# Order and SBUF byte offsets of the stationary tiles in the gate/up and q/k units of a fused decoder block

## Chip, cores and metric

The kernel runs on one core of a Trainium2 chip. The metric is the device time of one execution in microseconds (us). Three timed executions of the kernel before gave 1644.78, 1644.87 and 1646.24 us, so the median is 1644.87 us.

## What is computed

One decoder block on 256 tokens and 2048 channels, all in float32. The parts that matter here are the projections that make q and k of both attention branches, and the gated MLP:

```python
proj = x @ w_in                       # columns: GLA q/k/v/gate, FoX q/k/v, merge gates
...
def conv_gated_mlp(x, w_gate, w_up, conv_w, conv_b, w_down):
    g = causal_dwconv(x @ w_gate, conv_w, conv_b)
    h = jax.nn.gelu(g) * (x @ w_up)
    return h @ w_down
```

`w_gate` and `w_up` are 2048 x 5632. The q and k columns of `w_in` that concern us are 4 x 1024.

## The kernel before, in words

**Precision by parts.** Every float32 weight and activation is split into a high part (rounded to the matmul's fp32r format) and a low part (the rest). A product is taken as high x high + high x low + low x high. ScalarE makes the high part of a weight block with one copy (L132), VectorE makes the low part with one subtraction (L256).

**Units.** The weights come from HBM in units of 128 x 2048 floats, 284 of them, numbered u in the order in which they are used. `prep` loads a unit as two halves, and makes two high tiles and two low tiles of 128 x 1024. It runs three units ahead of the use. The high tiles rotate through six buffers of the pool `rhi`, the low tiles through six of `rlo`; each buffer has 1088 columns, 64 more than a tile, and the function `place(u)` says at which column the tile begins in its buffer (high, low). A column has 4 bytes. So `place` alone sets the byte offset of the tiles, and nothing else moves with it.

**Stationary weights.** Two kinds of units use the weight tiles as the stationary operand (the one that LDWEIGHTS loads): the 32 q/k units (u = 0 to 31) and the 88 gate/up units of the MLP (u = 136 to 223, gate and up in turn, so that odd u are up). All others use them as the moving operand. `w_unit` does one such unit. For each of 16 blocks of 128 weight rows (kts) there is a high matmul, L321: stationary high weights, moving 512 columns (256 high activations and 256 low ones); and a low matmul, L326: stationary low weights, moving the 256 high activations, added to the second half of the same PSUM bank. I call a high and the low behind it a pair. Each matmul comes with its own weight load, which the profile shows as PEld.

**The turn.** A unit whose number is in `TURN` has another order: six pairs, then the ten remaining lows in a row, then the ten remaining highs in a row. Before, this is unit 139 alone, the first gate/up unit behind the three units 136 to 138, which the step after the first LayerNorm does in another way (`w_phase`).

**Order around it.** In the q/k stage a `tick` in the middle of each unit lets one step of the attention or of the GLA levels put a few small matmuls or transposes between the pairs. In the MLP stage nothing stands between the units on TensorE: each gate or up unit is followed at once by the next. ScalarE and VectorE evict the PSUM bank, make the convolution, GELU and product (L363, L1458 to L1486), and the conversions of coming units.

Offsets in bytes before: q/k units 96 (high) and 240 (low); units 136 to 138 0 and 64; unit 139 0 and 208; units 140 to 223 64 and 16; all others 0 and 0. The program's tile addresses begin at a multiple of 256 bytes in every buffer, and the moving activations do too.

Of the kernel before, what the change touches and what calls it, by code (L numbers as in the profile page):

```python
# [35 lines left out]
GAPS = (96, 64, 80)  # L36


TURN = (139,)


def place(u):
    if u < 32:
        return 24, 60
    if u < 136 or u >= 224:
        return 0, 0
    if u < 139:
        return 0, 16
    return (0, 52) if u in TURN else (16, 4)


P_STAT = 5000
# [37 lines left out]
def tile_block(ctx: ExitStack, tc: tile.TileContext, wu, wfv, wpp, xT_in, x_in, pT_in, wlr,  # L90
# [28 lines left out]
    def t1(name):  # L119
        return sm.tile([P, 256], F32, tag="t1", bufs=6, name=name)  # L120
# [43 lines left out]
    def lo_tile(u, name):  # L164
        o = place(u)[1]
        return rlo.tile([P, 1088], F32R, tag="lo", name=f"lo{name}")[:, o:o + 1024]

    def hi_tile(u, name):
        o = place(u)[0]
        return rhi.tile([P, 1088], F32R, tag="hi", name=f"hi{name}")[:, o:o + 1024]  # L170
# [144 lines left out]
    def w_unit(ps, hi, lo, act, kts, first, last, tick=None):  # L315


        n = len(kts)

        def high(i, end=False):  # L320
            nc.tensor.matmul(ps, lhsT=hi[i // 8][:, i % 8 * P:i % 8 * P + P],  # L321
                             rhs=act[kts[i] // 4][:, kts[i] % 4, :], start=first and i == 0,
                             stop=last and end)

        def low(i, end=False):
            nc.tensor.matmul(ps[:, 256:512], lhsT=lo[i // 8][:, i % 8 * P:i % 8 * P + P],  # L326
                             rhs=act[kts[i] // 4][:, kts[i] % 4, 0:256], start=False,
                             stop=last and end)

        turn = n_used[0] - 1 in TURN  # L330
        pairs = 6 if turn else n
        for i in range(pairs):
            high(i)
            low(i, i == n - 1)
            if tick is not None:
                tick(i)
        for i in range(pairs, n):
            low(i)
        for i in range(pairs, n):
            high(i, i == n - 1)  # L340

    def w_phase(ps, hi, lo, act, t, kts, part=slice(None)):

# [141 lines left out]
    for u in range(8):  # L485
        hi, lo = fvu[u]
        for j in range(2):
# [8 lines left out]
            for t, i, c in seq:  # L496
                o, n = fch[c]
# [35 lines left out]
    for t in range(2):  # L533
        for c, (o, n) in enumerate(fch):
            n = min(n, 1024 - o)
# [143 lines left out]
    for n in range(16):  # L679
        h, j = n // 2, n % 2  # L680
        hi, lo = unit()

        ps = (mxtile if n == 0 else mmtile)(f"psf{'qk'[j]}{h}")
        w_unit(ps, hi, lo, xT, range(16), True, True,
               tick=lambda i: pull(1) if i == 7 else None)
        if n % 8 == 0:
            fqk[h // 4] = s8([P, 4, 2, 256], name=f"fqk{h // 4}")
        comb(ps, fqk[h // 4][:, h % 4, j], (P ** -0.5, 1.0)[j])
        if n >= 1:
            pull(1, parks)  # L690
# [105 lines left out]
    for n in range(16):  # L796
        nm, dst, sc = (("q", gq, 1.0 / 16.0), ("k", gk, 1.0))[n // 2 % 2]
        h, c = n // 4, n % 2
        hi, lo = unit()
        ps = mmtile(f"ps{nm}{2 * h + c}")  # L800
        w_unit(ps, hi, lo, xT, range(16), True, True,
               tick=lambda i: pull(1, mixers if n < 4 else levels) if i == 7 else None)
        comb(ps, dst[:, h, :].rearrange("p (t c n) -> p t c n", t=2, c=2)[:, :, c, :], sc)
        if n >= 4:
            pull(1)
        if n >= 1:
            pull(1, parks)
# [346 lines left out]
    for n in range(PSM1, 32):  # L1154
        if n in (26, 28):
            i = n // 2 - 13
# [282 lines left out]
    def gate_up(name):  # L1439
        if first:  # L1440
            return first.pop(0)
        hi, lo = unit()
        ps = mmtile(name)
        w_unit(ps, hi, lo, x1T, range(16), True, True)
        return ps

    for n in range(NF):
# [18 lines left out]
        u = t1("up")  # L1466
# [318 lines left out]
```

## Time and profile before

| | us |
|---|---|
| median of three timed executions | 1644.87 |
| the profiled execution, its own time | 1644.61 |
| its span, first to last instruction | 1642.8 |
| q/k units, first high matmul to the first of the next stage | 54.1 to 247.1 |
| gate/up units by `w_unit`, first to last | 847.0 to 1318.8 |

The page gives busy shares and the chain of waits that ends last; a busy TensorE is not a TensorE at its peak, because matmuls overlap. What tells the speed of a stretch that TensorE fills without a gap is the distance from the start of one matmul to the start of the next like it, read from the timeline, whose first column is the start in us from the span's begin and whose second is the duration.

### The profile page before, as it was taken

The numbers are of one execution on the slowest core, as the hardware profiler recorded it, in microseconds if no ns is written. First come the engines' busy times: TensorE is split into PE (matmuls) and PEld (weight loads), VectorE is DVE, ScalarE is ACT, GpSimd is POOL, SyncE is SP. The second block draws the span as 40 slices with busy tenths as digits, with TensorE's granted clock in tenths as the row PEclk, the third lists the DMA queues.
The fourth block names the chain that finished last, engine by engine and source line by source line (L and its number), as shares of the span: only waits on it lengthen the run. The fifth ranks groups of instructions, "written<-read, shape, count | busy, mean of one in ns | idle before, by whom it ended". The sixth has DMA issues, their size and how long they took to land.

```text
span 1642.8 us, 23489 instructions
## 1 busy us (share of the span) xinstructions
PE 1636.9 (100%) x8422; PEld 1402.9 (85%) x8422; DVE 1356.2 (83%) x1964; ACT 910.6 (55%) x1277; POOL 91.2 (6%) x244
## 2 busy tenths in 40 slices
PE   9999999999999999999999999999999999999998
PEld 9988888888888888888898888888888888888887
DVE  7687899788989857779987888888877688988787
ACT  6655555456666654446564444555555456566554
POOL 0000000000000000000010111110111000000000
PEclk9999999999999999999999999999999999999999
DMA  8799799878888768889756898888776679899474
GB/s 325 285 370 346 288 380 361 294 262 307 306 332 306 247 203 310 302 333 373 290 198 195 311 335 319 315 308 302 272 245 216 207 264 335 310 352 350 160 261 157
DMA packets 114838, 477.81 MB, mean 291 GB/s; under 512 B 13032, under 2 KB 14320, under 8 KB 95136
## 3 DMA queue, kind: packets, MB, share of 16 engines
q1 hardware_dynamic: 105216, 417.57, 71.2%
q0 software_dynamic: 9504, 58.73, 9.0%
q8 instruction: 66, 1.08, 0.2%
q14 instruction: 52, 0.43, 0.1%
HBM read 417.53 MB, written 58.73 MB: 290 GB/s over the span
## 4 chain that ended last, share of the span: by engine, by line
PE 99%; DVE 0%; ACT 0%; POOL 0%; issue 0%; ACTq 0%
PE psm L1006 11%; PE dn L868 10%; PE psu L321 10%; PE psg L321 9%; PE psa L1006 5%; PE psu L326 5%; PE psg L326 5%; PE dn_p L868 4%; PE wo L868 3%; PE gr L868 3%; PE gv L868 3%; PE fv L499 3%; PE pg L380 3%; PE psb L1006 3%; PE gr_p L868 2%; PE gv_p L868 2%
## 5 line engine op out<-in xcount | busy, mean ns | idle before, releaser
L256 DVE TENSOR_TENSOR lo<-raw,hi 128x1024 fp32r<-128x1024 f32 x456 | 551.7, 1220 | 138.5 <-ACT hi L132 137.2
L132 ACT ACTIVATE hi<-raw 128x1024 fp32r<-128x1024 f32 x456 | 476.9, 1057 | 301.7 <-DMA raw<-in_wu_dram 70.9
L321 PE MATMUL psu<-x1T,hi 128*128 128x512 f32 x688 | 239.5, 392 | 0.0
L321 PE MATMUL psg<-x1T,hi 128*128 128x512 f32 x672 | 234.9, 392 | 0.0
L326 PE MATMUL psu<-x1T,lo 128*128 128x256 f32 x688 | 191.3, 280 | 0.0
L326 PE MATMUL psg<-x1T,lo 128*128 128x256 f32 x672 | 188.6, 281 | 0.0
L1006 PE MATMUL psm<-hi,xT 128*128 128x512 f32 x512 | 163.1, 393 | 0.0
L321 PEld LDWEIGHTS psu<-x1T,hi 128*128 128x128 f32 x688 | 129.2, 188 | 28.2
L321 PEld LDWEIGHTS psg<-x1T,hi 128*128 128x128 f32 x672 | 126.2, 188 | 27.6
L132 ACT ACTIVATE hi_b<-raw 128x512 fp32r<-128x512 f32 x112 | 93.4, 842 | 71.6 <-DMA raw<-in_wu_dram 21.6
L326 PEld LDWEIGHTS psu<-x1T,lo 128*128 128x128 f32 x688 | 128.6, 188 | 0.0
L326 PEld LDWEIGHTS psg<-x1T,lo 128*128 128x128 f32 x672 | 126.2, 188 | 0.4 <-DVE lo L256 0.3
L230 DVE TENSOR_TENSOR lo_b<-raw,hi_b 128x512 fp32r<-128x512 f32 x112 | 105.1, 953 | 16.7 <-ACT hi_b L132 16.4
L174 DVE TENSOR_TENSOR td<-td 128x512 f32<-128x512 f32 x172 | 117.8, 685 | 0.9
L1006 PEld LDWEIGHTS psm<-hi,xT 128*128 128x128 f32 x512 | 96.3, 188 | 19.5
L230 DVE TENSOR_TENSOR lo_t<-td,hi_t 128x1024 fp32r<-128x1024 f32 x86 | 101.7, 1220 | 12.9 <-ACT hi_t L132 12.1
L132 ACT ACTIVATE hi_t<-td 128x1024 fp32r<-128x1024 f32 x86 | 88.1, 1053 | 28.0 <-DMA td<-td 15.5
L1006 PE MATMUL psm<-lo,xT 128*128 128x512 f32 x256 | 99.9, 390 | 0.0
L868 PE MATMUL dn<-hi,hC 128*128 128x512 f32 x352 | 97.9, 389 | 0.0
L1006 PE MATMUL psa<-hi,oT 128*128 128x512 f32 x256 | 81.2, 392 | 0.0
L868 PEld LDWEIGHTS dn<-hi,hC 128*128 128x128 f32 x352 | 66.0, 188 | 13.7
L1006 PEld LDWEIGHTS psa<-hi,oT 128*128 128x128 f32 x256 | 48.1, 188 | 9.9
(414 smaller groups left out, 3128.8 us busy)
## 6 DMA issues: line engine op xcount, KB each, us to landing
raw<-in_wu_dram SPq DMA_DIRECT2D x525, 512.0 KB, 6.2
td<-in_wu_dram SPq DMA_DIRECT2D x43, 1024.0 KB, 8.9
td<-td POOLq DMA_DIRECT2D x43, 1024.0 KB, 7.5
td<-td SPq DMA_DIRECT2D x43, 1024.0 KB, 8.0
hS<-sd SPq DMA_DIRECT2D x11, 1024.0 KB, 8.7
raw<-in_wu_dram SPq DMA_DIRECT2D x43, 256.0 KB, 7.7
fvraw<-in_wfv_dram SPq DMA_DIRECT2D x13, 524.0 KB, 6.9
sd<-hs POOLq DMA_DIRECT2D x24, 256.0 KB, 5.6
```

Of the source, the lines that this page charges most:

```text
L132: return nc.scalar.activation(o, i, AF.Copy, bias=0.0, scale=scale)
L174: sub = lambda o, a, b: nc.vector.tensor_tensor(o, a, b, ALU.subtract)
L230: nc.vector.tensor_tensor(lo, src, hi.bitcast(F32), ALU.subtract)
L256: i = nc.vector.tensor_tensor(lo, raw, hi.bitcast(F32), ALU.subtract)
L321: nc.tensor.matmul(ps, lhsT=hi[i // 8][:, i % 8 * P:i % 8 * P + P], rhs=act[kts[i] // 4][:, kts[i] % 4, :], start=first and i == 0, stop=l ...
L326: nc.tensor.matmul(ps[:, 256:512], lhsT=lo[i // 8][:, i % 8 * P:i % 8 * P + P], rhs=act[kts[i] // 4][:, kts[i] % 4, 0:256], start=False, s ...
L380: nc.tensor.matmul(bs[j][:, 0:m], lhsT=x, rhs=v[:, o:o + m], start=first and i == 0, stop=last and i == 2)
L499: nc.tensor.matmul(fbk[t][c][:, 0:n], lhsT=x, rhs=w[:, o:o + n], start=kt == 0 and i == 0, stop=kt == 15 and i == 2)
L868: nc.tensor.matmul(ps[:, e], lhsT=x, rhs=w, start=k == 1, stop=k == total.get(id(ps), 3 * ns))
L1006: nc.tensor.matmul(ps[t], lhsT=x, rhs=v, start=first and i == 0 and j == 0, stop=last and i == 3 and j == 2)
```

## The change

`place` gives the q/k units the offsets of the MLP units: 64 and 16 bytes. `TURN` becomes every fourteenth unit from 139 to 223: 139, 153, 167, 181, 195, 209 and 223, all of them up units. Their tiles stand at 0 and 240 bytes. And the end of a turn has another order: nine lows in a row, ten highs in a row, and then the last low.

```diff
-TURN = (139,)
+TURN = range(139, 224, 14)
 def place(u):
-    if u < 32:
-        return 24, 60
-    if u < 136 or u >= 224:
+    if 32 <= u < 136 or u >= 224:
         return 0, 0
-    if u < 139:
+    if 136 <= u < 139:
         return 0, 16
-    return (0, 52) if u in TURN else (16, 4)
+    return (0, 60) if u in TURN else (16, 4)
...
         for i in range(pairs):
             high(i)
             low(i, i == n - 1)
...
-        for i in range(pairs, n):
+        for i in range(pairs, n - 1):
             low(i)
         for i in range(pairs, n):
-            high(i, i == n - 1)
+            high(i)
+        if turn:
+            low(n - 1, True)
```

On TensorE, unit 139 (an up unit, PSUM tile psu1) ends before like this, and unit 140 (psg2) begins; hi139_0 is the first of its two high tiles, lo139_1 the second of its low tiles, and x1T0 to x1T3 are the four activation tiles:

```order
L326 MATMUL psu1_8057<-x1T1_7632,lo139_0_7830 128x256 x3
L326 MATMUL psu1_8057<-x1T2_7633,lo139_1_7836 128x256 x4
L326 MATMUL psu1_8057<-x1T3_7634,lo139_1_7836 128x256 x4
L321 MATMUL psu1_8057<-x1T1_7632,hi139_0_7828 128x512 x2
L321 MATMUL psu1_8057<-x1T2_7633,hi139_1_7834 128x512 x4
L321 MATMUL psu1_8057<-x1T3_7634,hi139_1_7834 128x512 x4
L321 MATMUL psg2_8109<-x1T0_7631,hi140_0_7860 128x512
L326 MATMUL psg2_8109<-x1T0_7631,lo140_0_7862 128x256
```

The same place in the changed kernel (the lines are two lower):

```order
L324 MATMUL psu1_8057<-x1T1_7632,lo139_0_7830 128x256 x3
L324 MATMUL psu1_8057<-x1T2_7633,lo139_1_7836 128x256 x4
L324 MATMUL psu1_8057<-x1T3_7634,lo139_1_7836 128x256 x3
L319 MATMUL psu1_8057<-x1T1_7632,hi139_0_7828 128x512 x2
L319 MATMUL psu1_8057<-x1T2_7633,hi139_1_7834 128x512 x4
L319 MATMUL psu1_8057<-x1T3_7634,hi139_1_7834 128x512 x4
L324 MATMUL psu1_8057<-x1T3_7634,lo139_1_7836 128x256
L319 MATMUL psg2_8109<-x1T0_7631,hi140_0_7860 128x512
L324 MATMUL psg2_8109<-x1T0_7631,lo140_0_7862 128x256
```

One low matmul has moved behind the ten highs, so that unit 140 now follows a low and not a high.

Unit 153 (psu8), before, has sixteen pairs; here are its ninth pair, its last, and the first of unit 154 on TensorE:

```order
L321 MATMUL psu8_8868<-x1T2_7633,hi153_1_8736 128x512
L326 MATMUL psu8_8868<-x1T2_7633,lo153_1_8738 128x256
...
L321 MATMUL psu8_8868<-x1T3_7634,hi153_1_8736 128x512
L326 MATMUL psu8_8868<-x1T3_7634,lo153_1_8738 128x256
L321 MATMUL psg9_8924<-x1T0_7631,hi154_0_8801 128x512
L326 MATMUL psg9_8924<-x1T0_7631,lo154_0_8803 128x256
```

In the changed kernel it ends as a turn:

```order
L324 MATMUL psu8_8868<-x1T1_7632,lo153_0_8732 128x256 x3
L324 MATMUL psu8_8868<-x1T2_7633,lo153_1_8738 128x256 x4
L324 MATMUL psu8_8868<-x1T3_7634,lo153_1_8738 128x256 x3
L319 MATMUL psu8_8868<-x1T1_7632,hi153_0_8730 128x512 x2
L319 MATMUL psu8_8868<-x1T2_7633,hi153_1_8736 128x512 x4
L319 MATMUL psu8_8868<-x1T3_7634,hi153_1_8736 128x512 x4
L324 MATMUL psu8_8868<-x1T3_7634,lo153_1_8738 128x256
L319 MATMUL psg9_8924<-x1T0_7631,hi154_0_8801 128x512
L324 MATMUL psg9_8924<-x1T0_7631,lo154_0_8803 128x256
```

Nine of its low matmuls have moved ahead of ten of its highs; the number of matmuls is the same. Units 167, 181, 195, 209 and 223 change in the same way. On ScalarE three conversions change places with a neighbour, on VectorE two; GpSimd and the DMA queue of SyncE keep their order.

## The prediction

> **What bounds the kernel now.** I read the page first: the first rows, the clock row and the chain of waits that ended last.
>
> ```profile
> span 1642.8 us, 23489 instructions
> ...
> PE 1636.9 (100%) x8422; PEld 1402.9 (85%) x8422; DVE 1356.2 (83%) x1964; ACT 910.6 (55%) x1277; POOL 91.2 (6%) x244
> ...
> PEclk9999999999999999999999999999999999999999
> ...
> PE 99%; DVE 0%; ACT 0%; POOL 0%; issue 0%; ACTq 0%
> ```
>
> TensorE is never without work, its clock is granted in full, and 99% of the chain is TensorE. So time can only come from how closely the matmuls follow each other. A group's mean duration doesn't tell that, since matmuls overlap; the timeline does, by the starts. In the MLP, from unit 157 (the first rows) to the last pair of unit 223:
>
> ```profile
> 947.21 0.39 PE L321 MATMUL psu<-x1T,hi 128*128 128x512 f32 x1
> 947.44 0.28 PE L326 MATMUL psu<-x1T,lo 128*128 128x256 f32 x1
> 947.56 0.39 PE L321 MATMUL psu<-x1T,hi 128*128 128x512 f32 x1
> ...
> 1318.49 0.39 PE L321 MATMUL psu<-x1T,hi 128*128 128x512 f32 x1
> ```
>
> 67 units of 16 pairs begin between these, so the first and last high are 1071 pairs apart: 371.28 / 1071 = 346.7 ns a pair, without one break. The q/k stage has the same pairs with other byte offsets (96 and 240). Two of its stretches, each with 23 pairs from the first row to the second:
>
> ```profile
> 238.90 0.39 PE L321 MATMUL psk<-xT,hi 128*128 128x512 f32 x1
> ...
> 246.80 0.39 PE L321 MATMUL psk<-xT,hi 128*128 128x512 f32 x1
> ...
> 223.84 0.40 PE L321 MATMUL psq<-xT,hi 128*128 128x512 f32 x1
> ...
> 231.92 0.39 PE L321 MATMUL psq<-xT,hi 128*128 128x512 f32 x1
> ```
>
> The first takes 7.90 / 23 = 343.5 ns a pair, the second 8.08 / 23 = 351.3 ns, with the same instructions, shapes and offsets. So a run of pairs settles into one of several rhythms and keeps it until something breaks in; offsets and the place where it starts decide which. This is all that the change can touch: 1408 pairs altogether, where 1 ns is 1.4 us.
>
> **The change part by part.** No matmul, load or conversion is added or removed. Four effects are left.
>
> *The q/k offsets.* By the starts, 128 of the 512 pairs lie in stretches like the second and the rest in stretches like the first, so the mean is 0.75 x 343.5 + 0.25 x 351.3 = 345.5 ns. What 64 and 16 bytes give, the MLP shows. The run to look at is the one where this rhythm was broken and began anew:
>
> ```profile
> 941.78 0.19 PEld L326 LDWEIGHTS psg<-x1T,lo 128*128 128x128 f32 x1 [0.35 <-DVE lo L256]
> ...
> 942.01 0.39 PE L321 MATMUL psg<-x1T,hi 128*128 128x512 f32 x1
> ...
> 943.40 0.39 PE L321 MATMUL psg<-x1T,hi 128*128 128x512 f32 x1
> ```
>
> At 941.4 TensorE waited 0.35 us for a low tile. The four pairs from 942.01 took 1.39 us, 347.5 ns each, and by 947.21 the 346.7 ns was back. So I take 346.7 for q/k too: 512 x 1.2 ns = +0.6 us. Each of the 32 units is broken in the middle by the other stage's matmuls, and a restart cost under 0.01 us here: 0.2 us more. Bounds: all pairs at 351.3 would be 512 x 5.8 = +3.0 us; all at the least I can build, below, -2.8 us.
>
> *The form of the turn.* Unit 139 and what follows it, before:
>
> ```profile
> 847.05 0.39 PE L321 MATMUL psu<-x1T,hi 128*128 128x512 f32 x1
> ...
> 848.34 0.28 PE L326 MATMUL psu<-x1T,lo 128*128 128x256 f32 x1
> 848.45 0.40 PE L321 MATMUL psu<-x1T,hi 128*128 128x512 f32 x1
> ...
> 849.03 1.45 PE L326 MATMUL psu<-x1T,lo 128*128 128x256 f32 x11
> 850.31 2.46 PE L321 MATMUL psu<-x1T,hi 128*128 128x512 f32 x10
> 852.61 0.39 PE L321 MATMUL psg<-x1T,hi 128*128 128x512 f32 x1
> ...
> 853.30 0.39 PE L321 MATMUL psg<-x1T,hi 128*128 128x512 f32 x1
> ...
> 854.35 0.39 PE L321 MATMUL psg<-x1T,hi 128*128 128x512 f32 x1
> ...
> 858.16 0.39 PE L321 MATMUL psu<-x1T,hi 128*128 128x512 f32 x1
> ...
> 863.71 0.39 PE L321 MATMUL psg<-x1T,hi 128*128 128x512 f32 x1
> ```
>
> The turn unit takes 852.61 - 847.05 = 5.56 us, the next 5.55, the one after 5.55, against 16 x 346.7 = 5.547. The lows in a row come every (850.31 - 849.03) / 11 = 116 ns, the ten highs every 230. So six new turns, each with the restart behind it, cost about 6 x 0.02 = +0.1 us. Moving one low to the end changes nothing in that sum. How a row at 240 bytes in place of 208 goes is not in the trace: the bounds are the pairs' own, 16 x (351.3 - 346.7) = +0.07 us and about as much below nothing, for each of seven turns: +-0.5 us. I take 208's value, the nearest.
>
> *The rhythm behind a turn.* This is the large term: units 140 to 223 without the six new turns are 78 units, 1248 pairs, and each now follows, somewhere ahead of it, a turn that ends on a low. Where these settle is not shown by any row, as no row has this start. The bounds: slow, 351.3, is +4.6 ns a pair, +5.7 us. Fast: the shortest distances seen are 113 ns for a low (848.34 to 848.45, to two digits) and 227 ns for a high in runs without lows (below), 340 ns in all, -6.7 ns a pair, -8.4 us; with the q/k pairs at 340, 512 x 5.5 = -2.8 us.
>
> ```profile
> 604.06 0.39 PE L1006 MATMUL psa<-hi,oT 128*128 128x512 f32 x1
> ...
> 625.82 0.39 PE L1006 MATMUL psb<-hi,ofTr 128*128 128x512 f32 x1
> ```
>
> (96 matmuls of 512 columns in 21.76 us: 226.7 ns each.) Between the bounds I take no change, 346.7, because the trace has two starts of this offset pair, one behind ten highs (852.61: five pairs in 1.74 us, 348 ns, and then 346.7) and one behind a wait that left the pairs out of step (942.01), and both end in the same rhythm within some four pairs. It seems to draw in whatever starts near it.
>
> *Tiles kept longer.* In a turn the first high tile is read until pairs 7 and 8 of the highs row, behind nine lows: 6 x 0.347 + 9 x 0.116 + 2 x 0.23 = 3.6 us into the unit instead of 8 x 0.347 = 2.8. So its buffer comes free 0.8 us later, for the ScalarE copy of the unit three further on. That copy's group over the MLP, and the only row in the list of TensorE's waits over the span:
>
> ```profile
> L132 ACT ACTIVATE hi<-raw 128x1024 fp32r<-128x1024 f32 x168 | 176.0, 1057 | 104.0 <-issue 41.6 <-DMA raw<-in_wu_dram 39.7 <-PE psu L321 15.9
> ...
> PE warm_ps L142 <- DVE warm L139: 1.2, 1, 1.2
> ```
>
> ScalarE does wait for up units' tiles (15.9 us in all), but it converts three units ahead, 3 x 5.5 us, and the list of TensorE's own waits holds nothing but the start; the only late tile is that of 941.8. The unit that was late there is 156, which is three behind the new turn 153. But its copy was not held by a buffer: it stood behind a GELU copy on ScalarE that waited for VectorE.
>
> ```profile
> 939.11 0.42 ACT L1464 ACTIVATE yc<-yc 128x256 f32<-128x256 f32 x1 [2.71 <-DVE yc L1463]
> 939.43 2.94 ACT L132 ACTIVATE hi<-raw 128x1024 fp32r<-128x1024 f32 x3
> ```
>
> So the cover holds; if it didn't, that wait would grow from 0.35 to at most 1.2 us. The few neighbours that change places on ScalarE and VectorE are one instruction of about 1 us each and are hidden in the same way. I put this at nothing, with +0.8 us as the upper bound.
>
> **The sum:** +0.6 + 0.2 + 0.1 = +0.9 us on the profiled execution's own 1644.61 (span 1642.8 and 1.8 around it), 1645.5. The median of the runs shown lies 0.26 us higher, so the forecast for a median is 1645.6 to 1645.8; I take 1645.6. What a measurement of this kernel can tell from no change is about 0.2%, 3.3 us, so this counts as within it.
>
> **A rule against the change.** The trace shows 343.5, 346.7 and 351.3 ns for the same pair. The Trainium skill, TensorE: Matmul & The Clock Gate, Part 2 (the step on LDWEIGHTS), says that TensorE has two independent SBUF read ports and that loading the next weights takes no read bandwidth from the running matmul. By that rule a tile's byte offset could not matter and the whole change would be worth 0, where the rows give +0.9; the trace speaks against it as far as these rhythms go, since only starts and offsets differ.
>
> **The rivals.**
>
> *Offsets and order without effect.* The rhythm depends on something else (the activations' place, say), and q/k and MLP keep what they have: 1644.6. For it: the MLP's spacing is the same in 67 units. Against: q/k, with other offsets, never shows 346.7. Chance 0.04; it falls within 0.2%.
>
> *A shorter rhythm behind the new turn.* The pair that follows a low rather than a high starts at another point of the rhythm, and the MLP may settle at q/k's 343.5: 1248 x 3.2 = -4.0, with q/k at 343.5 throughout -1.0, together 1639.7. Or at the floor of 340: -8.4 - 2.8 = 1633.4, with q/k left at 346.7 some 1637. For it: at q/k the same offsets hold two rhythms and the start chooses, so a second one for 64 and 16 is well possible, and a turn that is repeated would bring it back if it were lost. Against: two starts out of two went to 346.7. Chance 0.20 for the first size, 0.15 for the second.
>
> *A longer rhythm (slower).* The same mechanism chooses the slow one: behind a turn the pairs settle at 351.3 as q/k does in a quarter of its pairs, and, as the MLP has no break that would end it, they stay there for up to 13 units until the next turn starts them the same way. Price +5.7 us, 1650.3; with q/k slow as well (+3.0) 1653.3. It decides from 3.3 / 0.0046 = 720 pairs on, 45 of the 78 units, that is, if four of the seven turns fall into it. Chance 0.15.
>
> **How the numbers follow.** The forecast has 0.46, the rule's rival 0.04: within 0.2% together 0.50. Faster is 0.20 + 0.15 = 0.35, slower 0.15. The likeliest case's own range is 1643.5 to 1648, from the +-0.5 of the turns, the 0.8 of the tile wait and q/k between -1.0 and +1.5 (half of its pairs slow). The range for 8 in 10 takes in that case, the rule's rival and both sizes of the shorter rhythm, 0.85, and leaves out the slow one: 1633.5 to 1648.5.
>
> **What would show it.** In the changed kernel's timeline: unit 140 to 152, 13 units from the first high of psg2 to that of the turn, should take 13 x 5.547 = 72.1 us; 71.4 is the 343.5 rhythm, 70.7 the floor, 73.1 the slow one. The q/k stretch of 23 pairs from the 16th on should take 7.97 us instead of 7.90 or 8.08. Each of the new turns should take 5.56 us. The wait of 0.35 us at unit 156 should stay the only one. I am wrong if the units behind the new turn settle elsewhere than 346.7: then the start decides and not the offsets alone.

## The result and the profile after

| | before, us | changed, us |
|---|---|---|
| median of six executions | 1644.82 (1644.42 to 1646.24) | 1637.54 (1635.25 to 1639.82) |
| the profiled execution, its own time | 1644.61 | 1637.74 |
| its span | 1642.8 | 1635.9 |
| q/k units, first high to the first matmul of the next stage | 196.1 | 195.6 |
| gate/up units 139 to 223 | 471.8 | 465.15 |

The changed kernel takes 0.9952 of the time before, 95% interval 0.9939 to 0.9965: 7.3 us faster. The forecast of 1645.6 us was not met; the second size of the rival "a shorter rhythm behind the new turn", some 1637 us, lies nearest. Of the 6.9 us that the span lost, 6.6 lie in the gate/up units. (The first high matmul of the q/k units begins at 51.1 us in the kernel before, not at the 54.1 of the table ahead of the prediction; hence the 196.1.)

These are the first rows, the clock row, the chain of waits and two of the costliest groups on the page of the changed kernel. A group's row ends with the idle time ahead of it and what ended it.

```profile
span 1635.9 us, 23491 instructions
...
PE 1629.3 (100%) x8422; PEld 1396.6 (85%) x8422; DVE 1356.9 (83%) x1964; ACT 909.5 (56%) x1277; POOL 91.2 (6%) x244
...
PEclk9999999999999999999999999999999999999999
...
PE 96%; DVE 2%; DMA 1%; ACT 1%; issue 0%; POOL 0%; SPq 0%; ACTq 0%; DVEq 0%; POOLq 0%
...
L324 PE MATMUL psg<-x1T,lo 128*128 128x256 f32 x672 | 186.2, 277 | 0.6 <-DVE lo L254 0.6
```

Nothing on this page says why it is faster. TensorE has the same 8422 matmuls, the same full clock, and is again busy for all of the span. What is new is that the chain leaves TensorE for a while: from the one wait of the last row, at unit 156, it goes back over VectorE and ScalarE to a weight DMA at 900 us. The speed must again be read from the starts. This is the timeline of TensorE in the changed kernel, with the start and the duration in us in the first two columns: the last highs of turn 139, its single low, the first pairs of unit 140 (852.29), and then the first high of units 153, 154, 156, 157, 167, 168 and the last high of unit 223.

```profile
849.90 2.44 PE L319 MATMUL psu<-x1T,hi 128*128 128x512 f32 x10
852.17 0.28 PE L324 MATMUL psu<-x1T,lo 128*128 128x256 f32 x1
852.29 0.39 PE L319 MATMUL psg<-x1T,hi 128*128 128x512 f32 x1
852.51 0.28 PE L324 MATMUL psg<-x1T,lo 128*128 128x256 f32 x1
852.63 0.39 PE L319 MATMUL psg<-x1T,hi 128*128 128x512 f32 x1
...
923.01 0.39 PE L319 MATMUL psu<-x1T,hi 128*128 128x512 f32 x1
...
928.54 0.39 PE L319 MATMUL psg<-x1T,hi 128*128 128x512 f32 x1
...
939.42 0.39 PE L319 MATMUL psg<-x1T,hi 128*128 128x512 f32 x1
940.43 0.39 PE L324 MATMUL psg<-x1T,lo 128*128 128x256 f32 x1 [0.63 <-DVE lo L254]
...
945.87 0.39 PE L319 MATMUL psu<-x1T,hi 128*128 128x512 f32 x1
...
1001.34 0.39 PE L319 MATMUL psu<-x1T,hi 128*128 128x512 f32 x1
...
1006.88 0.39 PE L319 MATMUL psg<-x1T,hi 128*128 128x512 f32 x1
...
1311.55 0.39 PE L319 MATMUL psu<-x1T,hi 128*128 128x512 f32 x1
```

Units 140 to 152 take 923.01 - 852.29 = 70.72 us for 208 pairs, 340.0 ns each: the floor of the prediction, from the first pair on. Turn 153 takes 5.53 us. At 940.43 a low tile of unit 156 is late, 1.01 us behind the high at 939.42 where 0.23 is usual; unit 156 takes 6.45 us, and the ten units behind it run at 55.47 / 160 = 346.7 ns, the rhythm of before. Turn 167 (1001.34, 5.54 us) brings the 340.0 back, and it then lasts to the end.

In the q/k stage of the same timeline, a stretch of 30 pairs and one of 23:

```profile
129.13 0.39 PE L319 MATMUL psfq<-xT,hi 128*128 128x512 f32 x1
...
139.33 0.39 PE L319 MATMUL psfq<-xT,hi 128*128 128x512 f32 x1
...
238.60 0.40 PE L319 MATMUL psk<-xT,hi 128*128 128x512 f32 x1
...
246.59 0.39 PE L319 MATMUL psk<-xT,hi 128*128 128x512 f32 x1
```

10.20 / 30 = 340.0 ns and 7.99 / 23 = 347.4 ns: the same two rhythms (the second stretch needs a few pairs to settle at 346.7). By the trace's starts, 143 of the 458 pairs in stretches of more than ten have the first.

### The profile page after: what moved, and what is told of

It reads as the page before. It is cut to its first block, busy times and chain, and to the rows that moved or that the text cites. A ratio compares the mean times of both kernels' runs of the same rounds, so it can differ in the third digit from the quotient of the medians.

```text
span 1635.9 us, 23491 instructions
## 1 busy us (share of the span) xinstructions
PE 1629.3 (100%) x8422; PEld 1396.6 (85%) x8422; DVE 1356.9 (83%) x1964; ACT 909.5 (56%) x1277; POOL 91.2 (6%) x244
## 4 chain that ended last, share of the span: by engine, by line
PE 96%; DVE 2%; DMA 1%; ACT 1%; issue 0%; POOL 0%; SPq 0%; ACTq 0%; DVEq 0%; POOLq 0%
PE psm L1006 11%; PE dn L868 10%; PE psu L319 9%; PE psg L319 8%; PE psa L1006 5%; PE psu L324 4%; PE psg L324 4%; PE dn_p L868 4%; PE wo L868 3%; PE gr L868 3%; PE gv L868 3%; PE pg L380 3%; PE psb L1006 3%; PE fv L499 2%; PE gr_p L868 2%; PE gv_p L868 2%
## 5 line engine op out<-in xcount | busy, mean ns | idle before, releaser
L319 PE MATMUL psg<-x1T,hi 128*128 128x512 f32 x672 | 231.2, 390 | 0.0
L319 PE MATMUL psu<-x1T,hi 128*128 128x512 f32 x688 | 230.2, 390 | 0.0
L324 PE MATMUL psu<-x1T,lo 128*128 128x256 f32 x688 | 180.5, 277 | 0.0
L324 PEld LDWEIGHTS psu<-x1T,lo 128*128 128x128 f32 x688 | 125.3, 188 | 0.6
L172 DVE TENSOR_TENSOR td<-td 128x512 f32<-128x512 f32 x172 | 118.3, 688 | 0.9
```

The source lines that it names most:

```text
L172: sub = lambda o, a, b: nc.vector.tensor_tensor(o, a, b, ALU.subtract)
```

## The experiments

Times are medians where several executions ran, and single executions where one is named. In a single execution with seven turns, each of the six turns that have units behind them is a trial of its own. "MLP" is the stretch from the first matmul of unit 139 to the first behind unit 223, before 471.8 us, changed 465.15. Diffs are against the changed kernel unless said otherwise.

### Which of the two edits: the q/k offsets or the turns

**e1_qk_old**, the turns without the q/k edit:

```diff
+    if u < 32:
+        return 24, 60
```

> The changed kernel with the q/k units back at 96 and 240 bytes. If the two edits are independent: q/k stage 196.1 us as before (195.6 in the changed kernel, 0.45 less), mean uninterrupted pair 345.4 instead of 344.6 ns; MLP about 465 us. If the MLP's gain needs the q/k edit (a state carried on): MLP about 471.8.

Measured (one execution): 1639.9 us; q/k 196.15 us, MLP 465.75.

**e2_qk_alone**, against the kernel before, the q/k edit without the turns:

```diff
-        return 24, 60
+        return 16, 4
```

> The kernel before with the q/k units at 64 and 16 bytes and nothing else. Independent edits: q/k stage about 195.6 us, 0.45 less than before, its pairs a mixture of 340.0 and 346.7 ns; MLP 471.8 us as before, span about 1642.4 us. Rival, the prediction's own step: every q/k pair at 346.7, the stage 0.6 us longer than before.

Measured (one execution): 1644.2 us; q/k 195.63 us, MLP 471.7. By the two stretches, the edits do not touch each other: the q/k offsets are worth 0.5 us, and the rest is the turns'. (Of the 2.2 us by which e1_qk_old is longer than the profiled execution of the changed kernel, half lies outside both stretches.)

### Where the short rhythm starts and where it ends

**e3_one_turn**:

```diff
-TURN = range(139, 224, 14)
+TURN = (139,)
```

> The changed kernel with the first turn alone (unit 139). Theory A (the turn only sets the point at which the pairs start; a run of pairs then keeps its 340.0 ns until something breaks in): units 140 to 155 take 5.440 us each, as in the changed kernel; after the wait at unit 156 the units take 5.547 us to the end, since no turn sets them anew. MLP 16 x 5.440 + 5.54 + 6.45 + 67 x 5.547 = about 470.7 us, against 471.8 before and 465.2 with seven turns; span about 1641.5 us. Theory B (a turn acts only on the units near it, 13 or so): the same up to unit 153, but the units go over to 5.547 by themselves without a wait. Theory C (the offsets of the q/k units or of the tiles made the gain, the further turns nothing): MLP 465 us.

Measured: 1643.4 us, ratio 0.9981 (0.9962 to 1.0000), but the ten executions form two groups: three at 1634.7 to 1636.4 and seven at 1642.7 to 1644.8. The profiled one (1643.4) has 5.44 us a unit from 140 to 155, 5.63 for unit 156, and 5.55 from there to 223. One new turn gives the rhythm, and the wait at unit 156 ends it. The other turns of the change are there to take it up again. The three fast executions, of which there is no trace, probably came out of that wait in the short rhythm.

**e7_no_turn**:

```diff
-TURN = range(139, 224, 14)
+TURN = ()
```

> The changed kernel with no turn at all; unit 139 has sixteen pairs at 64 and 16 bytes too. Theory A (the 340.0 ns rhythm needs a start set exactly, and 346.7 takes in all other starts): units of 5.547 us throughout, MLP about 471.7 us. Rival (the MLP falls into 340.0 by itself from time to time, as q/k does in a third of its stretches): some long run of units at 5.440 us.

Measured (one execution): 1636.7 us, below the median of the changed kernel and within its executions. Its timeline on TensorE: the first high of unit 140, the break in unit 156, the first high of unit 157 and the last of 223.

```profile
852.10 0.39 PE L319 MATMUL psg<-x1T,hi 128*128 128x512 f32 x1
...
940.85 0.40 PE L319 MATMUL psg<-x1T,hi 128*128 128x512 f32 x1
941.08 0.35 PE L324 MATMUL psg<-x1T,lo 128*128 128x256 f32 x1
941.27 0.40 PE L319 MATMUL psg<-x1T,hi 128*128 128x512 f32 x1
...
946.38 0.39 PE L319 MATMUL psu<-x1T,hi 128*128 128x512 f32 x1
...
1310.52 0.39 PE L319 MATMUL psu<-x1T,hi 128*128 128x512 f32 x1
```

Ahead of the break 88.75 us for 256 pairs, 346.7 ns; behind it 364.14 us for 1071 pairs, 340.0. Here the break was short (941.08 to 941.27, 0.19 us where a low usually takes 0.12), and it happened to put the pairs on the short rhythm. So a break is a new draw. This would also explain three of the 59 executions of the kernel before, which took 1637.2 to 1637.3 us while all others took 1644 and more; none of the three has a trace.

**e8_two_turns**, a second turn right behind the break:

```diff
-TURN = range(139, 224, 14)
+TURN = (139, 157)
```

> The changed kernel with two turns, at 139 and at 157, the unit behind the one at which TensorE waits. Theory A (the turn sets the start, and only a break ends the 340.0 ns): units 140 to 155 and 158 to 223 take 5.440 us, unit 156 some 6.4 with its wait; MLP about 463.6 us, 1.5 us less than with seven turns (10 units less at 5.547, which is 1.07 us, and five turns less at 0.093, which is 0.47); median about 1636.0 us, and the executions lie closer together than the 1635.3 to 1639.8 of the changed kernel. Rival (there are further breaks in many executions, which the later turns mend): median like the changed kernel's 1637.5 or above.

Measured: 1636.08 us (1635.05 to 1637.22), ratio 0.9943 (0.9930 to 0.9956), MLP 462.9. Units 140 to 155 and 158 to 223 take 5.44 us. As expected.

**e12_parks_later**. "Parked" steps are differences of weight tiles (L172) that VectorE makes beside the gate units and sends back to HBM; this starts them six gate units later, with one turn:

```diff
-        if n >= 4:
+        if n >= 10:
             pull(1, parks)
```

> The changed kernel with one turn (139) and VectorE's block differences for the down projection (L174 lines) beginning at the eleventh instead of the fifth gate unit, so that they don't meet the layer norm's affine steps. If the wait at unit 156 comes from that pile on VectorE: no wait, no break, and 340.0 ns from unit 140 to 223 with one turn; MLP 5.54 + 84 x 5.44 = 462.5 us, median about 1634.9 us. If it comes from something else (a late weight load, ScalarE's order): a wait at 156 as before, and then by chance 340.0 or 346.7: median about 1643, with some executions near 1635.

Measured: 1640.9 us (1637.7 to 1642.7). The break at 156 was gone, and units 140 to 210 took 5.44 us, but units 211 and 212 took 7.45 and 8.27: the chain of waits goes back from there over a weight load that landed at 1246.2 to a pile of steps on VectorE, so the pile had moved. TensorE waited twice, for 1.85 and 0.76 us, and the granted clock then fell to 0.50 (1250 to 1252 us), with pairs of 0.64 us for about 3 us. The parked steps are thus a part of what makes the wait at 156; whether the affine steps are too, this run does not say.

**e14_affine_spread_one** leaves the parked steps and spreads what they meet, the affine steps of the first LayerNorm (L1293), over every second gate unit, with one turn:

```diff
-TURN = range(139, 224, 14)
+TURN = (139,)
...
-        if n >= 4:
+        if n >= 4 and n % 2 == 0:
             pull(1)
```

> One turn at unit 139, and the affine steps of VectorE pulled at every second gate unit instead of every one. If the affine steps, meeting the parked steps, make the wait at unit 156, no row of the waits names a low tile there, units 140 to 223 stay at 5.440 us throughout, the MLP takes about 462.6 us and all executions lie within 1634.5 to 1636.5 us. If the wait has another cause it stays, the rhythm behind it is drawn anew, and the executions fall into two groups as with one turn alone (near 1635 and near 1643). If the pile only moves, as it did when the parked steps were moved, the wait and the slower units stand further on, and the time lies between.

Measured: **1634.76 us**, all six executions within 1634.21 to 1636.36, ratio 0.9948 (0.9928 to 0.9967; the runs of before beside it held two of the 1637 kind), MLP 462.5. This is the timeline of VectorE ahead of unit 156 in the changed kernel, with affine steps (z), a parked difference (td), the convolution (yc) and the low tiles (lo):

```profile
927.71 0.69 DVE L1293 TENSOR_TENSOR z<-z,lnb 128x512 f32<-128x512 f32 x1
928.31 0.69 DVE L172 TENSOR_TENSOR td<-td 128x512 f32<-128x512 f32 x1
...
935.01 0.69 DVE L1293 TENSOR_TENSOR z<-z,lnb 128x512 f32<-128x512 f32 x1
...
936.59 1.07 DVE L1463 SCALAR_TENSOR_TENSOR yc<-gp,chn,yc 128x256 f32<-128x256 f32 x2
939.15 3.50 DVE L254 TENSOR_TENSOR lo<-raw,hi 128x1024 fp32r<-128x1024 f32 x3 [1.50 <-ACT hi L130]
```

and in e14_affine_spread_one:

```profile
925.47 0.68 DVE L172 TENSOR_TENSOR td<-td 128x512 f32<-128x512 f32 x1
...
932.47 0.69 DVE L1293 TENSOR_TENSOR z<-z,lnb 128x512 f32<-128x512 f32 x1
...
935.08 0.42 DVE L363 TENSOR_TENSOR gp<-psg,tmp 128x256 f32<-128x256 f32 x1 [1.93 <-ACT tmp L130]
...
936.06 1.07 DVE L1463 SCALAR_TENSOR_TENSOR yc<-gp,chn,yc 128x256 f32<-128x256 f32 x2
937.05 1.22 DVE L254 TENSOR_TENSOR lo<-raw,hi 128x1024 fp32r<-128x1024 f32 x1
938.63 2.36 DVE L254 TENSOR_TENSOR lo<-raw,hi 128x1024 fp32r<-128x1024 f32 x2 [0.36 <-ACT hi L130]
```

With one affine step fewer here, VectorE gets through the pile earlier and even has to wait at 935.08 for an eviction; the first low tile of unit 156 starts at 937.05 instead of 939.15, and no low tile of the gate/up units is late any more. Its timeline on TensorE, first high of unit 140 and last of 223:

```profile
852.87 0.39 PE L319 MATMUL psg<-x1T,hi 128*128 128x512 f32 x1
...
1309.49 0.39 PE L319 MATMUL psu<-x1T,hi 128*128 128x512 f32 x1
```

456.62 us for 84 x 16 - 1 = 1343 pairs: 340.0 ns, from one turn, to the end.

**e13_affine_spread_two**, the same with `TURN = (139, 157)`:

> Turns at 139 and 157 with the affine steps spread as above. If the wait at unit 156 (0.3 us, and its unit at 5.77 in place of 5.44) goes, the time is that of two turns without it: 1636.1 less 0.3, 1635.8 us, and the second turn is superfluous. If the wait stays, 1636.1.

Measured: 1635.3 us (1634.5 to 1636.4), MLP 462.6. The second turn is superfluous without the break.

**e16_affine_spread_none**, the same with `TURN = ()`, so without turn and without break:

> No turn, and the affine steps spread as in e14_affine_spread_one, so that neither a turn nor a break stands in the MLP. If e7_no_turn came to the short rhythm only by its break, all 85 units take 5.55 us here, the MLP 85 x 5.547 = 471.5, the whole about 1643.8 in every execution, 9 us above e14_affine_spread_one. If the pairs find 340.0 ns by themselves, the time is that of e14_affine_spread_one, 1634.8.

Measured: 1644.65 us (ten executions, 1643.1 to 1646.4), ratio 0.9999 (0.9989 to 1.0009). Its timeline, the same two highs as above:

```profile
851.92 0.39 PE L319 MATMUL psg<-x1T,hi 128*128 128x512 f32 x1
...
1317.50 0.39 PE L319 MATMUL psu<-x1T,hi 128*128 128x512 f32 x1
```

465.58 / 1343 = 346.7 ns throughout. This kernel and e14_affine_spread_one differ in one unit of 88, unit 139 (its order, and its tiles at 64 and 16 bytes instead of 0 and 240), and by 9.9 us, 0.6%. That the order alone is enough, e6_turn_at_64_16 below shows. The pairs do not find 340.0 by themselves, and the spread of the affine steps alone is worth nothing.

### What in the form of the turn does it

**e4_high_last**, seven turns at 0 and 240 bytes with the old ending (ten lows, then ten highs):

```diff
-        for i in range(pairs, n - 1):
+        for i in range(pairs, n):
             low(i)
         for i in range(pairs, n):
-            high(i)
-        if turn:
-            low(n - 1, True)
+            high(i, i == n - 1)
```

> Seven turns at 0 and 240 bytes, but each ends as before the change: ten lows, ten highs, no low behind. Theory A (the last low at the end of the highs hands the common start on to the next unit): the units behind each turn take 5.547 us, MLP about 471.8 us as before the change, and the turns still cost. Theory C (repeating the turn or the offset 240 made the gain, the place of the last low nothing): units of 5.440 us, MLP about 465 us.

Measured (one execution): 1644.8 us, MLP 471.7; no turn out of seven gave the short rhythm. Its timeline, the highs of turn 139, the first high of unit 140 and that of 153:

```profile
850.61 2.46 PE L319 MATMUL psu<-x1T,hi 128*128 128x512 f32 x10
852.91 0.40 PE L319 MATMUL psg<-x1T,hi 128*128 128x512 f32 x1
...
925.03 0.39 PE L319 MATMUL psu<-x1T,hi 128*128 128x512 f32 x1
```

72.12 / 208 = 346.7 ns. I took from this that a low must stand behind the ten highs. One more run showed that this was too much.

**e15_high_last_64_16**, the same with the turns' tiles at 64 and 16 bytes like all others:

```diff
-    return (0, 60) if u in TURN else (16, 4)
+    return 16, 4
```

> Seven turns with the old ending, ten lows and then ten highs, and with the turns' tiles at 64 and 16 bytes like all others. If the order at the end of a turn decides (a low must stand between the ten highs and the pairs), the units behind a turn take 5.55 us as in e4_high_last, the MLP 471.7 and the whole about 1644.8. If the step from 0 to 64 bytes between two highs spoilt e4_high_last's start, the units behind a turn take 5.440, the MLP about 465 and the whole about 1637.

Measured (one execution): 1637.7 us, MLP 465.6; every turn with units behind it gave the short rhythm. The same rows of its timeline:

```profile
849.53 2.50 PE L319 MATMUL psu<-x1T,hi 128*128 128x512 f32 x10
851.87 0.40 PE L319 MATMUL psg<-x1T,hi 128*128 128x512 f32 x1
...
922.60 0.39 PE L319 MATMUL psu<-x1T,hi 128*128 128x512 f32 x1
```

70.73 / 208 = 340.0 ns, with a high directly behind ten highs. So the order at the end of the turn does not matter by itself. With the old ending, the place of the turn's tiles decides. The nearest reading is that a high tile at 64 bytes directly behind a high tile at 0 spoils the start; the low that the change puts between them mends it, and so do equal offsets. It is not shown apart, since the two runs move the turn's low tiles along with the high ones, and the highs in a row at 64 bytes come at other distances.

**e6_turn_at_64_16**, the change's ending with the turns at 64 and 16 (the same one-line diff on the changed kernel):

> The changed kernel with the turns' tiles at 64 and 16 bytes like those of all other MLP units; the order of the turns stays. If the order alone sets the start: units of 5.440 us behind each turn, MLP about 465 us, and the turn's own place is superfluous. If the highs come to the common start only with high tiles at 0, or the last low keeps it only at 240: 5.547 us, MLP about 471.8 us. In the 340 ns rhythm a low at 16 behind a high at 64 does keep the start, so I lean to the first.

**e5_low208**, the change's ending with the turns at 0 and 208 as before:

```diff
-    return (0, 60) if u in TURN else (16, 4)
+    return (0, 52) if u in TURN else (16, 4)
```

> The changed kernel with the turns' low tiles at 208 bytes, as unit 139 had before. Theory A with the offset (the last low must take 113.3 ns from the common start, which 240 bytes gives): at 208 it takes another time, about 116 ns as in the row of lows before, the next unit starts off the beat, and units take 5.547 us, MLP about 471.8. Theory A without the offset (only the order counts): 5.440 us, MLP about 465 us.

Measured (one execution each): e6_turn_at_64_16 1637.2 us with MLP 465.2, and e5_low208 1638.7 with 465.6; in both the units follow the changed kernel's pattern, with turns of 5.55 to 5.59 us in the first and of 5.54 in the second. With the low at the end the turn's own place is superfluous, and the move from 208 to 240 bytes does nothing for the rhythm.

**e10_four_highs**, a shorter turn:

```diff
-        pairs = 6 if turn else n
+        pairs = 12 if turn else n
```

> The changed kernel with short turns: twelve pairs, three lows, four highs, one low. In the changed kernel's first turn the highs in a row came every 232, 231, 227, 226 ns and were even from the third on; in the second turn they needed eight. Theory A (the row of highs must be long enough to come to the common start): most of the seven turns fail, and the units behind those take 5.547 us; one that starts well gives 5.440. Rival (any low behind a high at the end of a turn does it): all seven give 5.440 us, and MLP is shorter than 465.2 by up to 0.5 us, as a short turn costs less.

Measured (one execution): 1642.3 us, MLP 468.2. The first highs of units 140, 153, 154 and 156:

```profile
853.86 0.39 PE L319 MATMUL psg<-x1T,hi 128*128 128x512 f32 x1
...
924.58 0.39 PE L319 MATMUL psu<-x1T,hi 128*128 128x512 f32 x1
...
930.12 0.39 PE L319 MATMUL psg<-x1T,hi 128*128 128x512 f32 x1
...
941.22 0.40 PE L319 MATMUL psg<-x1T,hi 128*128 128x512 f32 x1
```

340.0 ns up to unit 153, then 11.10 / 32 = 346.9. Turns 139, 167 and 195, which came out of the long rhythm, gave the short one; 153, 181 and 209, which came out of the short one, lost it. In this run four highs lead from either rhythm into the other; in the changed kernel ten lead into the short one from both (turn 153 came out of the short one, turn 167 out of the long).

### Do the offsets of the pairs still matter

**e9_pairs_at_0_0**, the ordinary gate/up units and the q/k units at 0 and 0, the turns as in the change:

```diff
-    return (0, 60) if u in TURN else (16, 4)
+    return (0, 60) if u in TURN else (0, 0)
```

> The changed kernel with the MLP's ordinary units at 0 and 0 bytes (q/k units then stand at 0 and 0 as well); turns at 0 and 240 as they are. If the start alone carries the 340.0 ns: units of 5.440 us behind the turns. If the offset is needed to keep it: a stream of 256 column matmuls with all tiles at multiples of 256 bytes came every 120 ns in the kernel before, so a pair takes 226.7 + 120 = 346.7 ns and units 5.547 us, MLP about 471.8.

Measured (one execution): 1655.0 us, MLP 479.7. The first highs of units 168 and 181:

```profile
1013.15 0.40 PE L319 MATMUL psg<-x1T,hi 128*128 128x512 f32 x1
...
1086.64 0.40 PE L319 MATMUL psu<-x1T,hi 128*128 128x512 f32 x1
```

73.49 / 208 = 353.3 ns behind the same turn, more than I expected. A start is of use only with offsets that hold the rhythm. The Trainium skill, TensorE: Matmul & The Clock Gate, Part 2, gives TensorE two independent SBUF read ports, so that the load of the next weights takes no SBUF read bandwidth from the running matmul. It says nothing of byte offsets, and the rows here do not test the ports; they show that the place of the weights sets the start-to-start time all the same, since only byte offsets and the order of a few units differ between 353.3, 346.7 and 340.0 ns.

### Can q/k have it too

**e11_qk_highs**, two turns, and in each q/k unit five lows ahead of the other stage's matmuls and six highs behind them (the core of the diff):

```diff
+            for i in range(8, 13):
+                low(i)
+            tick(7)
+            for i in range(8, 14):
+                high(i)
+            low(13)
```

> Two turns as in the run at 139 and 157, and in the q/k units another order: five lows are taken in ahead of the interruption in the middle of a unit, and behind it six highs follow in a row, then a low and the last two pairs. Theory A (highs in a row set the start, whatever breaks in before): nearly all pairs of q/k go at 340.0 instead of a mean of 344.6; 512 x 4.6 ns less some 10 ns for each row of highs is 2.0 us less in the q/k stage, 193.6 us; median about 1634.0 us. Rival (six highs are too few, or the rows cost what the rhythm gains): q/k stage 195.6 us or more.

Measured: 1636.6 us (six executions, 1635.8 to 1644.3), q/k 196.14 us, 0.5 longer instead of 2.0 shorter. By the starts, more of the remaining pairs ran at 340, but there were only 314 of them left in stretches; the rows of highs and lows took back what these gained. In its profiled execution unit 156 took 5.44 us, without a wait, though no step of VectorE had been moved.

## Why the prediction was wrong, point by point

**What bounds the kernel**: right. TensorE's starts set the time in every experiment; others came in only at the wait at unit 156 and, in e12_parks_later, at units 211 and 212.

**The rhythm behind a turn**: this is the step that failed. I had bounded it by +5.7 and -8.4 us and took "no change", because two starts of these offsets had both ended at 346.7 ns and "it seems to draw in whatever starts near it". Both starts were bad samples. At 852.61 the first high of unit 140, at 64 bytes, stood directly behind a high at 0; e4_high_last and e15_high_last_64_16 show that with this ending the place of the turn's tiles led it to 346.7. The start at 942.01 was a draw at a break; e3_one_turn and e7_no_turn show that such a draw can go either way. Both rhythms hold once entered, for 1343 pairs without a slip in e14_affine_spread_one and e16_affine_spread_none, so a rhythm that holds for 67 units says nothing on whether another exists. The sum: 67 units at 5.440 instead of 5.547 us is -7.2 us, against the bound of -8.4.

**The chain from the change to this**: the low at the end is needed only where the turns stand at 0 bytes and the rest at 64 (e4_high_last); with all tiles at 64 and 16 both endings work (e6_turn_at_64_16, e15_high_last_64_16). The 240 bytes and the six further turns are not its cause; the six serve to bring the rhythm back behind the break at 156, and only the one at 167 did so.

**The q/k offsets**: the sign was wrong. +0.6 and +0.2 us were forecast from "all at 346.7", and -0.45 came, since 31% of the pairs settle at 340.0. It lies within its bounds. The 0.2 for restarts had no ground, since the same breaks stand in the kernel before.

**The form of the turn**: the new turns take 5.53 us, forecast 5.56. Against the 5.44 beside them they cost 6 x 0.093 = 0.6 us and not 0.1, because what they are compared with became faster.

**Tiles kept longer**: I put the term at nothing and its bound at +0.8. This is the changed kernel's wait, from the list of the weight loads' waits:

```profile
PEld psg L324 <- DVE lo L254: 0.9, 1, 0.9
```

Unit 156 takes 6.45 us where it took 5.85 before (0.35 of waiting): +0.6, within the bound. The larger price is one that I did not see: the wait ends the rhythm, and ten units lie in the long one, 10 x 0.107 = 1.1 us. e12_parks_later and e14_affine_spread_one show that the parked and the affine steps of VectorE are both needed for the wait; e11_qk_highs shows that they are not enough.

As far as the traces tell, it is not the tiles kept by turn 153 that make the wait longer. In the eleven profiled kernels with a wait or a late low tile at unit 156, its first low tile was ready 14.3 us after the start of one ScalarE copy ahead of it (926.06 in the changed kernel, 927.42 before). That copy came 13.1 to 13.5 us before unit 156 in the six that have a turn at 153 and units 140 to 152 at 340.0 ns, and 13.9 to 14.2 in the other five. In the six, the chain of waits that ends at the late low tile goes back beyond that copy, to a weight load that landed more than 8 us before turn 153 began (in the changed kernel at about 914.0, the turn at 923.0). What makes that load late stays open: with a turn at 153 unit 156 took 6.35 to 6.68 us in those six, but 5.55 in e4_high_last and 5.65 in e9_pairs_at_0_0, where all was slow; without that turn, and with the steps of VectorE where they were, it took 5.44 to 5.85 at either rhythm.

**The sum**: -7.2 (67 units) + 0.6 (unit 156) is -6.6, what the MLP lost (471.79 to 465.15); with -0.45 in q/k, -7.1 of the span's -6.9. The rival's "some 1637" had the floor right for 67 of its 78 units. That it came within 1 us is luck: the slow units cost it 1.2 us and the wait 0.6, and q/k, which it left at 0.8 longer, gave 1.25 back.

**A faster version than both**: e14_affine_spread_one, 1634.76 us, one turn and no break. Against the changed kernel it saves the wait (1.0 us), the ten slow units (1.1) and the six further turns (0.6): 2.7, measured in the MLP 2.65.

## What to carry to other kernels

Where a stretch is bound by TensorE and nothing waits, divide it by its pairs and compare with the sum of the shortest start-to-start distances seen anywhere in the trace: 346.7 against 227 + 113 was 2% over all gate/up units, and it was there to be had. A steady rhythm is no sign that it is the only one; change the byte offset of the stationary tiles, or the order of one unit at the start, and look at the starts again. Then keep breaks out of the stretch, since a wait of 0.1 us can cost 7 us behind it (in the traced execution of e3_one_turn one low came 0.09 us late, and 67 units behind it took 0.107 us more each), and time such a kernel many times, since one execution may be a lucky draw.

## What was not expected of the hardware

The settled distances of one and the same pair were 340.0, 343.3, 346.7, 351.1 and 353.3 ns; the first, third and fifth are 51, 52 and 53 times 6.67 ns, and the 226.7 ns of a 512-column matmul is 34 times that. What the 6.67 ns are, no run shows.

Starts that lead to different rhythms differ by a few ns. By the trace's starts, the second high of a stretch that entered the short rhythm took 226 to 229 ns to the next start (the changed kernel, e5_low208, e6_turn_at_64_16, e7_no_turn, e15_high_last_64_16), and 231 to 233 where the long one followed (before, e4_high_last, e3_one_turn behind its break). This one distance does not decide alone: behind the breaks of e1_qk_old and e5_low208 it was 229, and the long rhythm followed.

The ten highs need not be on the beat themselves: at 0 bytes they came every 227 ns by the end of the row, at 64 bytes they went on at 231 and 236 in turn (e6_turn_at_64_16, e15_high_last_64_16), and both led into 340.0.
